# Down projection with seven products of halves in three chunks of its contraction, in one sequence with gate/up and the embedding gate

## The chip, the cores and the metric

The kernel runs on one core of a Trainium2 chip. The metric is the device time of one execution in microseconds; the time given for a kernel is the median of its runs.

## What is computed

One decoder layer over 2048 tokens with a model width of 1024, all in float32. The part that matters here is the end of the layer. `h` is the residual after attention and mLSTM, `rms_norm` scales by the root of the mean square and by a gain:

```python
D_MODEL = 1024; SEQ = 2048; PLE_DIM = 256
D_FF = ((8 * D_MODEL + 3 * 256 - 1) // (3 * 256)) * 256      # 2816
...
mix = jnp.concatenate([mla_out, mlstm_out], axis=-1) @ w_out[i]
h = h + rms_norm(mix, attn_post_norm[i])
f = rms_norm(h, ffn_pre_norm[i])
f = (jax.nn.silu(f @ w_gate[i]) * (f @ w_up[i])) @ w_down[i]
h = h + rms_norm(f, ffn_post_norm[i])
h = h + jax.nn.sigmoid(h @ w_ple_gate[i]) * (p[i] @ w_ple_proj[i])
```

## The kernel before, in words

Tensors lie transposed: rows of 128 features on the partitions, tokens along the free axis, in four blocks of 512 tokens (b = 0 to 3). Two blocks form a token pair: `tb = 1` is blocks 2 and 3, which goes first, `tb = 0` is blocks 0 and 1. A float32 product is made of three matmuls on halves of the mantissa (`mm3`, L133 to L138): each operand is split into `hi` (a cast on ScalarE, L128) and `lo` (a subtraction on VectorE, L124, the line of the helper `tt`), for weights in the tiles `wh`/`wl`, for activations in `xh`/`xl`. One matmul is 128x128 by 128x512.

Gate and up are made as a 2x2 block product with seven products in place of eight (Strassen's scheme in Winograd's form): `strassen`, L352. The two rows of the block are gate tile j and up tile j, the two columns the token blocks of the pair, and the contraction is cut in two halves of 512. `w_ops` (L323) loads the four quarters of the weights of one j into `wr` tiles and forms the seven weight operands; `lead_first` and `lead_second` (L279, L292) form the seven activation operands, four 128x512 tiles each, which stay for all 22 j. One product (`step`, L367) is 4 tiles x 3 = 12 matmuls. The methods `p1` to `p7` order the seven products of one j among those of its neighbours; the partial sums go out of PSUM into `ct` tiles by ScalarE (`copy`, L384) or are added by VectorE (`result`). Since the activation operands of a new token pair are not ready when it starts, the first j of each pair of token blocks is made with eight plain products (`straight_pair`, L474) while VectorE forms the others. `gate_up` (L1452) multiplies silu(gate) by up and writes the result to DRAM (`hf`).

After both token pairs comes the down projection in `phase3` (from L1328): for each of the four token blocks the 22 tiles of `hf` are loaded and split, and each of the 8 output tiles takes 22 x 3 = 66 matmuls with freshly loaded and split weights. `second_norm` (L1443) normalises a block and writes the new residual to DRAM (`h2`). Then `embed` (L1477) makes the sigmoid gate with the same seven products for each token pair (4 row pairs of w_ple_gate, the first of them straight), with the small projection of p between them.

`first_norm` (in `phase3`) makes `h1` of a block after the output projection; for blocks 0 and 1 its eight steps per block stand in `self.side`, a list from which `tick` (L224) takes one step after each product of the running sequence. So this work lies beside the first j of `gate_up(1)`.

The order of instructions on each engine is set when the program is built: a scheduler simulates the program and places each instruction on its engine's list, and each engine then runs its list in that order. Tiles come from pools with a fixed number of buffers per name (`SHARED`, `OWN`, L38 and L39: five `ld`, seven `ct`, six `acc`, two `tt`, one `sq`, four `wr`, seven `wh` and `wl`, 28 `xh` and `xl`); a tile's first writer waits until a buffer of that name is free. All loads and stores named here are issued by SP.

Of the kernel before, what the change touches and what calls it, by code (L numbers as in the profile page):

```python
# [17 lines left out]
P = 128  # L18
D = 1024
T = 2048  # L20
TB = 512
# [13 lines left out]
BUSY = 4  # L35
# [26 lines left out]
class Layer:  # L62
# [13 lines left out]
    def setup(self):  # L76
# [41 lines left out]
        self.hf = [dt([KF, P, TB], F32, name=f"hf{b}") for b in range(NB)]  # L118
        self.y2 = [dt([KD, P, TB], F32, name=f"y2_{b}") for b in range(NB)]
        self.h2 = [dt([KD, P, TB], F32, name=f"h2_{b}") for b in range(NB)]  # L120
# [134 lines left out]
    def load(self, src, alt=False, tag=None):  # L255
        t = self.tl(tag or ("ct" if alt else "ld"))
        self.nc.sync.dma_start(out=t, in_=src)
        return t
# [20 lines left out]
    def lead_first(self, get, spare=False):  # L279

        st = self.xs = {}
        self.help = "dve"
        self.raws = {}
        self.ops = [[] for _ in range(7)]
        for n, k in enumerate(LEAD):
            x = self.raws[k] = get(k, 0, "ct" if n > 5 else "xl" if n % 2 else "xh")
            st[k, 0] = self.x_pair(x, "dve")
            self.ops[0 if k < 4 else 2].append(st[k, 0])  # L290

    def lead_second(self, get):  # L292
# [9 lines left out]
        def sums(kk):  # L302
# [7 lines left out]
            ops[4].append(self.x_pair(t1, self.help))  # L310
            tt("dve", b21, b21, t2, ALU.subtract)
            ops[5].append(self.x_pair(b21, self.help))
# [10 lines left out]
    def w_ops(self, w1, w2, busy, first):  # L323
# [8 lines left out]
        help = self.help if busy else "dve"  # L332
        tt("dve", s1, a21, a22, ALU.add)
        o0 = self.w_pair(a11, lo_eng=help)
        o2 = self.w_pair(a12, lo_eng=help)
# [11 lines left out]
        o5 = self.w_pair(a22, lo_eng=help)  # L347
# [3 lines left out]

    def strassen(self, xo, pairs, emit, lead, place=None, late=False):  # L352


        nc, tt = self.nc, self.tt

        def ct():
            return self.tl("ct")

        def prod(ps, w, x, kk, start, stop, onto=False):  # L360
            s = slice(kk * P, (kk + 1) * P)
            self.mm3(ps, (w[0][:, s], w[1][:, s]), x[kk], start, stop, onto)

        self.straight_pair(*pairs[0], lead, emit, place)
        state, order = {}, [None]

        def step(j, i, bank, first=True):  # L367

            wo = state[j]["w"]
            with ExitStack() if order[0] is None else self.tc.issue_after(order[0]):  # L370
                for kk in range(4):
                    with self.paced():
                        prod(bank, wo[i], xo[i], kk, first and kk == 0, kk == 3, not first)
            order[0] = self.last("PE")
            with self.behind():
# [6 lines left out]
        def copy(bank, c=None):  # L382
            c = c or self.tl("ct")
            nc.scalar.copy(out=c, in_=bank)  # L384
            return c

        def done(j, i, t, c):
            state[j]["out"].append((i, t, c))
            if late and len(state[j]["out"]) < 4:
                return  # L390
            for i, t, c in state[j]["out"] if late else [(i, t, c)]:
                emit(j, i, t, c)

        def where(j, i, t, c=None):
            return place and place(j, i, t) or c or self.tl("ct")

        def result(j, i, t, bank, x):
            c = where(j, i, t, x)
            tt("dve", c, bank, x, ALU.add)
            done(j, i, t, c)  # L400

        def p1(j):
            s = state[j] = dict(w=self.w_ops(*pairs[j], j < BUSY, j == 1), out=[])
            s["a"] = self.bank()
            step(j, 0, s["a"])
            s["c1"] = copy(s["a"])

        def p2(j):
            s = state[j]
            bank = self.bank()  # L410
            step(j, 2, bank)
            result(j, 0, 0, bank, s["c1"])

        def p6(j):
            s = state[j]
            step(j, 1, s["a"], False)
            s["u2"] = copy(s["a"])

        def p5(j):
            s = state[j]  # L420
            s["b"] = self.bank()
            step(j, 4, s["b"])
            if "p3" in s:
                tt("dve", s["u2"], s["b"], s["u2"], ALU.add)
                result(j, 0, 1, s["p3"], s["u2"])

        def p7(j):
            s = state[j]
            step(j, 3, s["a"], False)
            s["u3"] = copy(s["a"])  # L430
            if "b" in s:
                result(j, 1, 1, s["b"], s["u3"])

        def p4(j):
            s = state[j]
            step(j, 5, s["a"], False)
            done(j, 1, 0, copy(s["a"], where(j, 1, 0)))

        def p3(j):
            s = state[j]  # L440
            if "b" in s:
                step(j, 6, s["b"], False)
                result(j, 0, 1, s["b"], s["u2"])
            else:
                s["p3"] = self.bank()
                step(j, 6, s["p3"])


        final = len(pairs) - 1
        for f in (p1, p2, p3, p6, p5, p7):  # L450
            f(1)
        for j in range(2, final + 1):
            p1(j)
            p2(j)
            p4(j - 1)
            p6(j)
            if j < final:
                p5(j)
            if j > 2:
                p3(j - 1)  # L460
            p7(j)
# [4 lines left out]
        s = state[final]  # L466
        result(final, 1, 1, s["b"], s["u3"])
# [862 lines left out]
    def phase3(self):  # L1330
        nc, a, V = self.nc, self.a, self.vecs
        st = ExitStack()
        with st:
# [4 lines left out]
            self.h2_done = set()  # L1338
# [52 lines left out]
            def ready(b, r):  # L1391
                rf[b] = r
                if b >= 2:
                    self.lead_first(scaled(1), True) if b == 2 else self.lead_second(scaled(1))
# [9 lines left out]
            self.gate_up(1, self.ops, self.xs)  # L1404
# [201 lines left out]
```

## Time and profile before

| | |
|---|---|
| median of 3 runs | 2758.14 us (2758.07 to 2763.62) |
| profiled execution, its own time | 2755.9 us |
| its span | 2754.1 us |
| granted TensorE clock, mean | 0.983 |
| TensorE matmul busy | 2633.2 us, 96% of the span, 12307 instructions |
| VectorE busy | 1815.0 us, 66%, 3355 instructions |
| ScalarE busy | 1314.5 us, 48%, 2585 instructions |
| DMA | 386.93 MB, mean 140 GB/s |

A busy share is the time that instructions of an engine ran, over the span. Matmuls overlap in the pipeline, so their durations don't add up; how many start in a stretch is the better measure. The share of DMA is the mean busy share of the core's 16 DMA engines.

### The profile page before, as it was taken

To read this page: it belongs to the slowest core of one execution; us is meant where nothing else is said; L and a number is where in the kernel's file an instruction comes from. 1 tells how busy PE (TensorE), PEld (TensorE's weight loads), DVE (VectorE), ACT (ScalarE), POOL (GpSimd) and SP (SyncE) were. 2 spreads that over 40 slices of the span, in tenths; PEclk is the share of its full clock that TensorE was granted. 3 is DMA by queue.
4 is the path that set the end of the run, shared out by engine and by line. 5 is a ranking of instruction groups with operands and counts; after the bars stand their busy time and mean duration, and the time that the engine had idled before them with its cause. 6 is when DMAs were issued, how large, how long until landed. Compare 5 with 4: busy or idle time off the path is not lost.

```text
span 2754.1 us, 36357 instructions
## 1 busy us (share of the span) xinstructions
PE 2633.2 (96%) x12307; PEld 2183.3 (79%) x12307; DVE 1815.0 (66%) x3355; ACT 1314.5 (48%) x2585; POOL 185.6 (7%) x393
## 2 busy tenths in 40 slices
PE   7799889999999999999999989999999999999999
PEld 6678668778888878878888877888888888888777
DVE  8987877566666653898555585555573454646996
ACT  5565565466555543465333354433352334434463
POOL 0010010244333100000000000000000000000000
PEclk9899999999999999999999999999999999999999
DMA  4345354743432144737222232222263565756552
GB/s 141 125 160 194 122 148 149 223 123 96 126 104 88 55 161 161 248 105 236 81 84 83 82 123 81 87 82 81 84 213 114 178 223 178 258 164 229 183 161 84
DMA packets 222822, 386.93 MB, mean 140 GB/s; under 512 B 26252, under 2 KB 39180, under 8 KB 222636
## 3 DMA queue, kind: packets, MB, share of 16 engines
q1 hardware_dynamic: 221292, 383.59, 42.9%
q8 instruction: 96, 1.57, 0.2%
q10 hardware_dynamic: 1344, 1.03, 0.1%
q14 instruction: 90, 0.74, 0.1%
HBM read 278.48 MB, written 106.04 MB: 140 GB/s over the span
## 4 chain that ended last, share of the span: by engine, by line
PE 79%; DVE 8%; DMA 7%; ACT 3%; issue 2%; POOL 1%; SPq 0%; DVEq 0%; POOLq 0%; ACTq 0%
PE ps L136 22%; PE ps L137 22%; PE ps L138 22%; PE ps_t L1300 2%; DMA wr<-g_rd 1%; DVE xl L124 1%; PE ps_o L137 1%; DVE ct L124 1%; DVE wl L124 1%; PE ps_s L1260 1%; PE ps_o L138 1%; PE ps_o L136 1%; PE ps_s L1261 1%; PE ps_s L1262 1%; PE ps_s L1263 1%
## 5 line engine op out<-in xcount | busy, mean ns | idle before, releaser
L136 PE MATMUL ps<-xh,wh 128*128 128x512 f32 x3000 | 1175.0, 395 | 49.2 <-ACT xh L128 18.6
L137 PE MATMUL ps<-xl,wh 128*128 128x512 f32 x3000 | 1178.9, 393 | 5.0 <-DVE xl L124 4.1
L138 PE MATMUL ps<-xh,wl 128*128 128x512 f32 x3000 | 1177.0, 393 | 0.0
L136 PEld LDWEIGHTS ps<-xh,wh 128*128 128x128 f32 x3000 | 569.3, 190 | 174.9 <-ACT xh L128 22.4
L137 PEld LDWEIGHTS ps<-xl,wh 128*128 128x128 f32 x3000 | 569.7, 190 | 125.3 <-DVE xl L124 5.9
L138 PEld LDWEIGHTS ps<-xh,wl 128*128 128x128 f32 x3000 | 569.2, 190 | 119.9 <-DVE wl L124 0.3
L124 DVE TENSOR_TENSOR wl<-wr,wh 128x512 fp32r<-128x512 f32 x575 | 387.0, 675 | 400.8 <-ACT wh L128 396.1
L128 ACT CAST wh<-wr 128x512 fp32r<-128x512 f32 x575 | 348.2, 608 | 632.8 <-PE ps L137 492.2
L124 DVE TENSOR_TENSOR ct<-ps,ct 128x512 f32<-128x512 f32 x174 | 120.0, 690 | 133.8 <-PE ps L138 127.8
L384 ACT COPY ct<-ps 128x512 f32<-128x512 f32 x248 | 144.0, 580 | 29.1 <-PE ps L138 21.8
L128 ACT CAST wh<-st 128x512 fp32r<-128x512 f32 x128 | 78.6, 620 | 163.4 <-PE ps L137 142.4
L128 ACT CAST xh<-ld 128x512 fp32r<-128x512 f32 x164 | 99.8, 621 | 64.4 <-DMA ld<-hf 28.8
L1311 DVE TENSOR_TENSOR acc<-ps_t,acc 128x512 fp32r<-128x512 f32 (+2 forms) x144 | 91.8, 643 | 53.3 <-ACT acc L1310 52.8
L1268 DVE TENSOR_REDUCE mx<-ps_s 128x1 f32<-128x512 f32 (+3 forms) x160 | 96.9, 608 | 35.6 <-PE ps_s L1264 33.4
L124 DVE TENSOR_TENSOR xl<-ld,xh 128x512 fp32r<-128x512 f32 x152 | 102.8, 690 | 20.4 <-ACT xh L128 19.6
L1310 ACT CAST acc<-ps_t 128x512 fp32r<-128x512 f32 (+2 forms) x144 | 78.0, 551 | 70.5 <-PE ps_t L1300 68.7
L1278 ACT ACTIVATE xl<-ps_s,mn 128x512 f32<-128x512 f32 (+3 forms) x144 | 90.3, 633 | 39.7 <-DVE mn L1274 23.0
L124 DVE TENSOR_TENSOR wl<-st,wh 128x512 fp32r<-128x512 f32 x128 | 87.7, 689 | 24.3 <-ACT wh L128 24.3
L1300 PE MATMUL ps_t<-ident,xl 128*128 128x128 f32 x544 | 88.3, 277 | 0.3 <-DVE acc L1311 0.3
L124 DVE TENSOR_TENSOR acc<-acc,sq 128x512 f32<-128x512 f32 x102 | 70.4, 691 | 12.9 <-ACT sq L249 12.4
L1300 PEld LDWEIGHTS ps_t<-ident,xl 128*128 128x128 f32 x544 | 68.6, 143 | 11.4 <-DVE acc L1311 0.5
L1260 PE MATMUL ps_s<-xh,wh 128*128 128x512 f32 (+2 forms) x160 | 66.8, 418 | 7.4 <-ACT xl L1278 7.2
(317 smaller groups left out, 3035.0 us busy)
## 6 DMA issues: line engine op xcount, KB each, us to landing
wr<-w_down SPq DMA_DIRECT2D x160, 256.0 KB, 2.9
wr<-w_gate SPq DMA_DIRECT2D x88, 256.0 KB, 2.8
wr<-w_up SPq DMA_DIRECT2D x88, 256.0 KB, 2.8
hf<-ct SPq DMA_DIRECT2D x88, 256.0 KB, 2.0
ld<-hf SPq DMA_DIRECT2D x88, 256.0 KB, 4.3
wr<-w_in SPq DMA_DIRECT2D x80, 256.0 KB, 3.1
y<-ct SPq DMA_DIRECT2D x64, 256.0 KB, 2.2
ld<-y SPq DMA_DIRECT2D x56, 256.0 KB, 4.1
```

Source lines behind the costliest of these rows:

```text
L124: (self.nc.gpsimd if eng == "pool" else self.nc.vector).tensor_tensor(out=out, in0=x, in1=y, op=op)
L128: self.nc.scalar.copy(out=hi, in_=src)
L136: mm(out, w[0], x[0], start=start, stop=False)
L137: mm(out, w[0], x[1], start=False, stop=False)
L138: mm(out, w[1], x[0], start=False, stop=stop)
L384: nc.scalar.copy(out=c, in_=bank)
L1260: mm(o, qn[0][:, qs], kn[c][0][:, :n], start=True, stop=False)
L1268: v.tensor_reduce(mx[:, j, c:c + 1], s_ps[:, :w], axis=AX.X, op=ALU.max, negate=True)
L1278: nc.scalar.activation(out=p[:, :x.shape[1]], in_=x, func=AF.Exp, bias=top, accum_out=sm[:, j, c:c + 1])
L1300: nc.tensor.transpose(t_ps[:, j * P:(j + 1) * P], pt[j, kt // 4][:, kc], self.ident)
L1310: nc.scalar.copy(out=ph[:, b0:], in_=t_ps[:, c0:])
L1311: v.tensor_tensor(pl[:, b0:], t_ps[:, c0:], ph[:, b0:].bitcast(F32), ALU.subtract)
```

## The change

- Down projection: the 22 contraction tiles are cut into three chunks of 2x3, 2x4 and 2x4 tiles (`CHUNKS`), and in each chunk two output tiles by two token blocks are made with seven products of halves. The 16 output tiles of a token pair stay in SBUF (`wr`, `ppl`, `ct`) over the three chunks, and the parts are added there.
- The weight operands of down and of the embedding gate are formed once (`w_sum`, 16 of them: 4 row pairs x 3 chunks of down, and 4 of w_ple_gate) and stored to DRAM as seven tiles each; each use loads them and splits them (`w_fed`). The 16 steps are appended to `self.side` before `gate_up(1)` starts.
- The activation operands of `gate_up(0)`, of down and of embed are formed once (`x_sums`) and stored to DRAM as seven tiles, with seven stores, in place of one store of each `hf`, `h2` tile; `fed` loads and splits them.
- `stream` runs gate/up of both token pairs, down of both (three jobs each) and embed of both as one sequence: while the last j of one job runs, the activation operands of the next are loaded, product by product. Only the first j of `gate_up(1)` is still made with eight plain products.
- `second_norm` becomes eight steps per token pair in `self.side`. The product of gate and up goes to `acc` (first token block) or `ppl` (second), not into the `ct` tile of the gate.
- `BUSY` and the variants of engine and spare go away without effect: both engines named were the same.

```diff
+CHUNKS = ((0, 3), (6, 4), (14, 4))
+FED = (0, 2, 1, 4, 3, 5, 6)
...
+    def w_sum(self, w1, w2, n, dst):
+        tt = self.tt
+        a11, a12, a21, a22 = (self.load(w[:, z * n:(z + 1) * n], n=n)[:, :n] for w in (w1, w2) for z in range(2))
+        s1, s2 = (self.tl("tt")[:, :n] for _ in range(2))
+        tt("dve", s1, a21, a22, ALU.add)
+        tt("dve", s2, s1, a11, ALU.subtract)
+        tt("dve", a21, a11, a21, ALU.subtract)
+        s4 = self.tl("sq")[:, :n]
+        tt("dve", s4, a12, s2, ALU.subtract)
+        for i, x in enumerate((a11, s2, a12, a21, s1, a22, s4)):
+            self.nc.sync.dma_start(out=dst[i][:, :n], in_=x)
+    def fed(self, hi, lo, src, n=TB):
+        hi, lo = self.tl(hi, F32R), self.tl(lo, F32R)
+        raw = lo.bitcast(F32)[:, :n]
+        self.nc.sync.dma_start(out=raw, in_=src)
+        self.nc.scalar.copy(out=hi[:, :n], in_=raw)
+        self.tt("dve", lo[:, :n], raw, hi[:, :n].bitcast(F32), ALU.subtract)
+        return hi, lo
+    def w_fed(self, src, n):
+        o = {i: self.fed("wh", "wl", src[i][:, :n], n) for i in FED}
+        return [o[i] for i in range(7)]
+    def x_sums(self, b11, b12, b21, b22, dst, t3, t4):
+        tt, dma = self.tt, self.nc.sync.dma_start
+        t1, t2 = self.tl("tt"), self.tl("tt")
+        dma(out=dst[0], in_=b11)
+        dma(out=dst[2], in_=b21)
+        dma(out=dst[6], in_=b22)
+        tt("dve", t1, b12, b11, ALU.subtract)
+        dma(out=dst[4], in_=t1)
+        tt("dve", t2, b22, t1, ALU.subtract)
+        dma(out=dst[1], in_=t2)
+        tt("dve", t3, b22, b12, ALU.subtract)
+        dma(out=dst[3], in_=t3)
+        tt("dve", t4, b21, t2, ALU.subtract)
+        dma(out=dst[5], in_=t4)
...
             order[0] = self.last("PE")
+            if id(jb) in after and j == len(jb["pairs"]) - 1:
+                feed(after[id(jb)], i)
             with self.behind():
                 self.tick()
...
+    def part(m, i, t, bank):
+            if not jb["sums"]:
+                c = self.tl("ct")
+                nc.scalar.copy(out=c, in_=bank)
...
             self.until(lambda: 3 in rf)
-            self.gate_up(1, self.ops, self.xs)
-            self.until(lambda: 1 in rf)
-            self.lead_first(scaled(0))
-            self.lead_second(scaled(0))
-            self.gate_up(0, self.ops, self.xs)
-            for b in (2, 3, 0, 1):
-                xs = [self.x_pair(self.load(self.hf[b][k])) for k in range(KF)]
...
+            self.side += self.weight_sums()
+            jobs = [self.gate_up(1, xo=self.ops, lead=self.xs),
+                    self.gate_up(0, feed=lambda i: [x[i] for x in self.h1op],
+                                 ready=lambda: self.h1_done == 4)]
             for tb in (1, 0):
...
+                jobs += self.down(tb)
+            self.stream(jobs + [self.embed(tb) for tb in (1, 0)])
...
                 s, u = half.pop((j, 0, t)), half.pop((j, 1, t))
-                self.tt("dve", s, u, s, ALU.mult)
-                nc.sync.dma_start(out=self.hf[2 * tb + t][j], in_=s)
...
+                x = got[j, t] = self.tl("ppl" if t else "acc")
+                self.tt("dve", x, u, s, ALU.mult)
+                m = j // 2
+                quad = [(k, z) for k in (2 * m, 2 * m + 1) for z in range(2)]
+                if all(i in got for i in quad):
+                    b = [got.pop(i) for i in quad]
+                    self.x_sums(*b, self.hfop[tb][m], b[1], self.tl("sq"))
...
+        def half(kk, z):
+            for t in range(2):
+                k, b = 4 * z + kk, 2 * tb + t
+                y, h = self.load(self.y2[b][k], tag="ld"), self.load(self.h1[b][k], tag="acc" if tb else "st")
+                nc.vector.scalar_tensor_tensor(y, y, V[:, 32 + k:33 + k], self.r2[tb, t], ALU.mult, ALU.mult)
+                self.tt("dve", y, y, h, ALU.add)
+                got[z, t] = y
+            if z:
+                b = [got[z, t] for z in range(2) for t in range(2)]
+                nc.sync.dma_start(out=self.h2op[tb][kk][7], in_=b[1])
+                self.x_sums(*b, self.h2op[tb][kk], self.tl("st"), self.tl("st"))
+                self.h2_done[tb] += 1
+        self.side += [lambda kk=kk, z=z: half(kk, z) for kk in range(4) for z in range(2)]
```

### What the change moves

Three places matter. All are at the start of `gate_up(1)`, where j = 3 and j = 4 of gate/up are under way. Numbers behind names tell tiles of one name apart; a line of the changed kernel differs from that of the one before (its L133 and L129 are the split's L128 and L124, its L456 the copy's L384, its L251 the first square of `square_sum`, L246).

**ScalarE, before.** The copy `ct_13101<-ps_13005` takes the second partial sum of j = 3 out of PSUM, before TensorE may go on into the same bank with the product `p7` of j = 3:

```order
L128 CAST wh_13188<-wr_13177 128x512
L249 ACTIVATE sq_12884<-ld_12877 128x512
L384 COPY ct_13075<-ps_12815 128x512
L128 CAST wh_13192<-wr_13179 128x512
L384 COPY ct_13101<-ps_13005 128x512
L249 ACTIVATE sq_12910<-ld_12903 128x512
```

**ScalarE, now.** The same copy is `ct_13509<-ps_13413`; `ld_13129` is the first tile of `first_norm` of block 0:

```order
L133 CAST wh_13609<-st_13593 128x512
L1544 ACTIVATE ct_13321<-ct_13321 128x512
L251 ACTIVATE acc_13105<-ld_13129 128x512
L456 COPY ct_13509<-ps_13413 128x512
L254 ACTIVATE sq_13159<-ld_13152 128x512
L254 ACTIVATE sq_13229<-ld_13222 128x512
L133 CAST wh_13614<-wr_13589 128x512
```

The copy now stands behind the first square of `first_norm` of block 0, which before came fifteen rows ahead of it.

**VectorE, now.** Behind the lower half of the fourth weight operand of j = 4 (`wl_13610`) come 41 rows of `w_sum` in a row, of the sixth sum to the last, without any other instruction between them. This is their end (`ld_13080`, `ld_13082`, `ld_13076`, `ld_13078` are the four quarters of the last sum):

```order
L129 TENSOR_TENSOR sq_13055<-ld_13044,tt_13050 128x512
L129 TENSOR_TENSOR tt_13084<-ld_13080,ld_13082 128x512
L1456 SCALAR_TENSOR_TENSOR ld_13129<-ld_13129,vecs_67,acc_13103 128x512
L129 TENSOR_TENSOR tt_13085<-tt_13084,ld_13076 128x512
L129 TENSOR_TENSOR ld_13080<-ld_13076,ld_13080 128x512
L129 TENSOR_TENSOR ld_13129<-ld_13129,ppl_13131 128x512
L129 TENSOR_TENSOR sq_13089<-ld_13078,tt_13085 128x512
L129 TENSOR_TENSOR tt_13286<-ppl_12911,acc_12684 128x512
L129 TENSOR_TENSOR acc_13283<-ct_13281,ct_12990 128x512
```

The tile that the first square of `first_norm` reads is written behind 43 of the 44 rows of the last eleven sums, and so is the product of gate and up of j = 1 (`acc_13283`), which frees two `ct` tiles.

**SP, now.** The eleven DMAs of one weight sum, as they stand in the middle of those eleven sums (a sum's seven stores and four loads of its neighbours; no load for gate/up is among them):

```order
L262 DMA ld_12782<-w_down 128x512
L262 DMA ld_12784<-w_down 128x512
L262 DMA ld_12812<-w_down 128x512
L365 DMA w_sums_down2_1_171<-ld_12780 128x512
L365 DMA w_sums_down2_1_171<-ld_12784 128x512
L365 DMA w_sums_down2_2_172<-ld_12812 128x512
L365 DMA w_sums_down2_1_171<-tt_12786 128x512
L365 DMA w_sums_down2_1_171<-tt_12787 128x512
L365 DMA w_sums_down2_1_171<-ld_12782 128x512
L262 DMA ld_12814<-w_down 128x512
L365 DMA w_sums_down2_1_171<-sq_12791 128x512
```

This group of eleven repeats; the four loads of each sum go through the five `ld` buffers, which the stores of the sum before must give back.

## Rows read from the trace of the kernel before

**Rows 1.** The page's engines and slices: busy share in 40 slices of 69 us.
```profile
span 2754.1 us, 36357 instructions
PE   7799889999999999999999989999999999999999
DVE  8987877566666653898555585555573454646996
PEclk9899999999999999999999999999999999999999
DMA  4345354743432144737222232222263565756552
```

**Rows 2.** Windows in gate/up and down: stretch, busy us (and instructions) by engine, clock, DMA.
```profile
1400.00:1450.00 50.00, 50.00 (x222) 41.40 (x222) 28.12 (x44) 19.88 (x35) 0.00 (x0) 1.00 0.25 84
1500.00:1550.00 50.00, 50.00 (x222) 41.42 (x221) 28.11 (x44) 19.53 (x34) 0.00 (x0) 1.00 0.25 82
2050.00:2100.00 50.00, 50.00 (x222) 41.43 (x221) 23.06 (x37) 18.46 (x32) 0.00 (x0) 1.00 0.56 177
2160.00:2560.00 400.00, 400.00 (x1787) 331.83 (x1786) 224.13 (x388) 153.03 (x267) 0.00 (x0) 1.00 0.63 205
```

**Rows 3.** Windows from the first token pair of gate/up to the second.
```profile
1600.00:1650.00 50.00, 42.77 (x180) 34.31 (x179) 44.63 (x72) 25.90 (x46) 0.00 (x0) 0.97 0.35 116
1650.00:1700.00 50.00, 45.00 (x188) 36.43 (x188) 30.67 (x49) 19.70 (x34) 0.00 (x0) 0.93 0.23 79
1655.00:1660.00 5.00, 3.44 (x8) 2.51 (x8) 4.29 (x8) 2.36 (x5) 0.00 (x0) 0.50 0.20 64
1660.00:1665.00 5.00, 5.00 (x22) 4.04 (x21) 1.89 (x3) 1.48 (x3) 0.00 (x0) 0.94 0.06 17
```

**Rows 4.** Windows of the embedding, to 4 us before the end.
```profile
2550.00:2600.00 50.00, 46.53 (x205) 37.46 (x203) 47.23 (x85) 24.27 (x44) 0.00 (x0) 1.00 0.50 159
2600.00:2650.00 50.00, 47.59 (x202) 38.98 (x203) 41.54 (x68) 26.09 (x47) 0.00 (x0) 0.97 0.74 241
2650.00:2700.00 50.00, 47.59 (x201) 38.47 (x200) 48.35 (x81) 30.72 (x56) 0.00 (x0) 0.97 0.38 123
2700.00:2750.00 50.00, 47.91 (x211) 39.12 (x209) 30.06 (x46) 18.87 (x33) 0.00 (x0) 1.00 0.15 56
```

**Rows 5.** Timeline of DVE, back to back.
```profile
1208.35 0.69 DVE L124 TENSOR_TENSOR wl<-wr,wh 128x512 fp32r<-128x512 f32 x1
1208.95 0.69 DVE L124 TENSOR_TENSOR tt<-ct,tt 128x512 f32<-128x512 f32 x1
1209.55 0.70 DVE L124 TENSOR_TENSOR ld<-ct,ld 128x512 f32<-128x512 f32 x1
```

**Rows 6.** Five of the 10 us windows with busiest DMA.
```profile
1090.00:1100.00 10.00, 10.00 (x46) 8.28 (x45) 5.61 (x10) 4.14 (x8) 0.00 (x0) 1.00 1.03 373
1130.00:1140.00 10.00, 10.00 (x46) 8.29 (x45) 7.08 (x11) 4.71 (x8) 0.00 (x0) 1.00 1.04 387
1240.00:1250.00 10.00, 10.00 (x46) 8.29 (x45) 9.07 (x16) 5.75 (x11) 0.00 (x0) 1.00 1.03 348
1250.00:1260.00 10.00, 10.00 (x46) 8.29 (x45) 10.00 (x17) 6.21 (x11) 0.00 (x0) 1.00 1.04 357
2370.00:2380.00 10.00, 10.00 (x46) 8.29 (x45) 6.80 (x11) 3.31 (x6) 0.00 (x0) 1.00 1.00 360
```

**Rows 7.** Timeline of PE: the statistics of blocks 0 and 1 among j = 1.
```profile
1206.34 1.84 PE L162 MATMUL psx<-rmean,acc 128*128 128x1 f32 x16
1208.05 0.49 PE L137 MATMUL ps<-xl,wh 128*128 128x512 f32 x1
```

**Rows 8.** The window of 50 us at the start of gate/up.
```profile
1200.00:1250.00 50.00, 50.00 (x234) 41.78 (x233) 46.87 (x96) 28.89 (x52) 0.00 (x0) 1.00 0.45 151
```

**Rows 9.** The chain that ended last, of the second norm: a store, then a load.
```profile
2575.24 2.01 DMA h<-ld
2577.32 3.39 DMA ld<-y
2580.73 0.75 DVE ld L1447
2594.82 3.33 DMA h<-ld
```

**Rows 10.** The page's DMA issues: KB each, us from issue to landing.
```profile
hf<-ct SPq DMA_DIRECT2D x88, 256.0 KB, 2.0
ld<-y SPq DMA_DIRECT2D x56, 256.0 KB, 4.1
```

More of the change, by code (lines that the diff above doesn't have):

```diff
@@ L397, in result @@
[L397 to L403, printed above, removed]
+        def part(m, i, t, bank):
+            jb, j = seq[m]
+            if not jb["sums"]:
+                c = self.tl("ct")
+                nc.scalar.copy(out=c, in_=bank)
+                state[m][i, t] = c
+                return
+            kind, tiles = jb["sums"]
+            if kind == "first" and (j, i, t) not in tiles:
+                c = tiles[j, i, t] = self.tl("wr" if j == 0 else "ppl" if j == 1 or (j, i, t) == (3, 1, 0) else "ct")
+                nc.scalar.copy(out=c, in_=bank)
+            else:
+                c = tiles[j, i, t]
+                tt("dve", c, bank, c, ALU.add)
@@ L404, in p1, with p2 @@
+        def p1(m):
+            jb, j = seq[m]
+            if j == 0 and jb["begin"]:
+                jb["begin"]()
+            s = state[m] = dict(w=jb["weights"](j, m == 0), out=[])
             s["a"] = self.bank()
[L405 to L409, printed above, removed]
+            step(m, 0, s["a"])
+            part(m, 0, 0, s["a"])
+        def p2(m):
             bank = self.bank()
-            step(j, 2, bank)
-            result(j, 0, 0, bank, s["c1"])
@@ L427, in p7 @@
[L427 to L430, printed above, removed]
-            if "b" in s:
[L432 to L440, printed above, removed]
+                x = s[0, 1]
+                tt("dve", x, s["b"], x, ALU.add)
+                whole(m, 0, 1, s["p3"])
@@ new lines, in down, with emit @@
+    def down(self, tb):
+        nc, tiles, accs, got = self.nc, {}, {}, {0: 0, 1: 0}
+        def emit(j, i, t, c):
+            b = 2 * tb + t
+            nc.sync.dma_start(out=self.y2[b][2 * j + i], in_=c)
+            if t not in accs:
+                accs[t] = self.acc_tile()
+            self.square_sum(accs[t], c, got[t] == 0, tag="tt")
+            got[t] += 1
+            if got[t] == KD:
+                self.rms_later(accs[t], 1024, lambda r: self.second_norm(tb, t, r))
+        jobs = []
+        for c, (k0, n) in enumerate(CHUNKS):
+            pairs = [self.down_pair(j, k0, n) for j in range(KD // 2)]
+            jobs.append(self.job(
+                pairs, emit, n=n, sums=("last" if c == 2 else "more" if c else "first", tiles),
+                weights=lambda j, first, c=c, n=n: self.w_fed(self.w_sums[f"down{c}", j], n * P),
+                feed=lambda i, k0=k0, n=n: [x[i] for x in self.hfop[tb][k0 // 2:k0 // 2 + n]]))
+        return jobs
@@ L1500, in steps, with begin @@
             turn = ((0, 0), (1, 0), (1, 1), (0, 1)) if j == 0 else ((0, 0), (1, 1), (1, 0), (0, 1))
[L1501 to L1504 removed]
+            return [lambda: weight(j)] + [lambda n=n, t=t: ahead(n, t) for n, t in turn]
+        def begin():
+            self.side += [lambda t=t, k=k: embed_in(t, k) for t in range(2) for k in range(2)] + steps(0)
         def emit(j, n, t, c):
```

284 lines of the change are left out of this document (158 added, 126 removed).

## Prediction

> **What bounds the kernel now.** I read the page first, then windows by stage, then the order of both programs. TensorE is busy from the start of the last third to the end at the full granted clock while VectorE and DMA have room [rows 1]. In a steady stretch of gate/up or of down 222 matmuls start in 50 us, so one costs 50/222 = 0.2252 us, and no other engine is near its limit [rows 2]. TensorE's list of matmuls is the bound there: a matmul that is left out is 0.2252 us off the time. It loses time at two places. Between the token pairs of gate/up 180 + 188 matmuls start in 100 us where 444 would fit, 76 x 0.2252 = 17.1 us, part of it at the lower clock after the gap (0.50, then 0.94) [rows 3]. In the embedding 819 start in 200 us where 888 would fit, 15.5 us, and the last row of windows stops 4 us before the end [rows 4].
>
> The sum is made against the profiled execution's own 2755.9 us, which is 2.2 us under the median of the runs, 2758.14.
>
> **What goes.** Down took 4 blocks x 8 tiles x 66 matmuls = 2112; now 2 token pairs x 4 row pairs x 7 products x 11 tiles x 3 = 1848, which is 264 fewer. Three first j lose their eighth product (`gate_up(0)` and both embeddings), 3 x 12 = 36. Together 300, at 0.2252 us **-67.6 us**. The gap between the token pairs goes almost wholly, since the operands of the next job are loaded during the last j of this one: **-15** of 17.1 [rows 3]. Of the embedding's 15.5 us [rows 4] I take **-12**; the tail of the last outputs stays. Without anything added: 2755.9 - 94.6 = 2661.3 us.
>
> **What is added beside TensorE.** VectorE's list from the first operand of down to the end of down holds 212 full and 28 three-quarter operations for the first token pair and 266 and 28 for the second. Back to back one takes 0.60 us [rows 5], so 142 and 174 us against 924 x 0.2252 = 208 us of matmuls per pair: covered on the whole, cost nothing, but with little room. If that cover were gone VectorE would set the pace of down. In gate/up it is busy 28 of 50 us [rows 2], and `x_sums` adds 4 operations per two j, 2.4 us in 38: covered. DMA in down and second norm is 63 MB in 208 us for the second token pair, 303 GB/s on the mean, where the busiest windows carried 348 to 387 at a share of 1.00 to 1.04 [rows 6]: covered on the mean, not in its bursts.
>
> **The weight sums: the term that decides.** The 16 steps of `w_sum` are in the side list ahead of `first_norm` of blocks 0 and 1 and come within 16 products. Buffers of one name are given out in program order as I read the lists, so the first `ld` and `acc` tiles of `first_norm` come behind all sums, and the `acc` tile for the product of gate and up of j = 1 behind those; its two `ct` tiles stay taken meanwhile. The scheduler's lists show the result: on ScalarE the copy that frees the bank for `p7` of j = 3 stands behind the first square of `first_norm`, and on VectorE that square's input stands behind 43 of the 44 operations of the last eleven sums. So TensorE can't start `p7` of j = 3 before nearly all sums are made. Nothing remains for it ahead of that: `wl_13610`, which stands on VectorE right before the eleven sums, needs a buffer that `p3` of j = 2 gives back, the product before `p7`. Behind the waiting copy are queued the casts of the weights of j = 4, and SP has no load for j = 5 but one until the sums are through.
>
> When would TensorE get there? Its list is the same up to the start of j = 1. The statistics at 1206.34 to 1208.05 us [rows 7] stand in the middle of its first product; from there 17 products and 2 matmuls, 206 x 0.2252 = 46.4 us, lead to about 1255 us. In the trace of before nothing waits there [rows 8].
>
> How long do eleven sums take? Two bounds. By volume: from the second load of the sixth sum to the last load of the sixteenth SP has 114 DMAs, 29.9 MB; at 387 to 348 GB/s [rows 6] 77 to 86 us. By the chain of a buffer: a load 3.39 to 4.1, three operations of 0.60 until the third quarter may be stored, a store 2.0 to 3.33 [rows 5, 9, 10], 7.2 to 9.2 us for one sum, since four of the five `ld` buffers go round in each; ten rounds are 72 to 92. Both limits act on the same transfers, so I take 8.5 us a round, near the upper end because the latencies in those rows were met at less than full DMA: 85 us, and 5 for the first sum's and the last sum's own operations and the square and copy behind them. **+90 us**, ends 72 and 105 (ten rounds of 10).
>
> The page "DMA: Bandwidth & Descriptors" of the Trainium skill, section Bandwidth, speaks against this change: it gives 138 GB/s for transfers of 64 KB and 341 for 1 MB and asks for 1 MiB or more, which for the 256 KB pieces here would put the rate between the two and make these 29.9 MB an estimated 88 to 217 us. The trace doesn't agree: with several in flight the same pieces ran at 348 to 387 [rows 6], so the rows decide. The same section has 425 GB/s for 16 MB, by which the stall would be some 70 us; no row here reaches that.
>
> **Smaller terms.** After such a gap the clock comes back as in [rows 3], +2 us. Then VectorE has the 16 steps of `first_norm` and the products that piled up, beside j = 4 and 5; before, the same steps lay there with VectorE busy 46.87 of 50 us [rows 8] and no gap: +6, ends 0 and 15. `second_norm` of the first token pair lies under chunks 0 and 1 of the second pair's down: 101 DMAs, 26.1 MB, with 18 weight operands among them; 73 us at 357 GB/s, against 198 matmuls, 44.6 us, and one row pair loaded ahead, 14 us: **+15**, ends 0 and 30. The other five changes of operands: 28 loads, casts and subtractions beside 14 products, 11 MB in 38 us, 290 GB/s: +6 in all, ends 0 and 20. `second_norm` of the second token pair must end before the last embedding starts: 102 DMAs, 26.7 MB, 75 us, against some 53 us of matmuls after its second statistic: **+15**, ends 5 and 25.
>
> Sum: 2661.3 + 90 + 2 + 6 + 15 + 6 + 15 = **2795.3**, I say 2795 us, 1.3% over the median. With all low ends 2661.3 + 72 + 2 + 0 + 0 + 0 + 5 = 2740; with all high ends 2661.3 + 105 + 2 + 15 + 30 + 20 + 25 = 2858.
>
> **The rivals.**
> *A, the sums are quick.* If loads and stores run ahead far enough, the eleven sums go at VectorE's pace: 44 x 0.60 = 26 us, and the time is 2661.3 + 26 + 44 = 2731; with the smaller terms at their low ends too, 2661.3 + 26 + 7 = 2694. It decides when the block takes less than 94.6 - 44 = 51 us, 4.6 us a sum. For it: DMA was idle for half of this stretch [rows 8], so the first five sums may be done early. Against: 4.6 us a sum are 2.88/4.6 = 626 GB/s, which no row comes near. Faster than before; 0.16, of which I see more near 2730 than below.
> *B, transfers slower than the busiest windows.* If a sum's stores and loads wait for each other through the five buffers, so that a round takes 12 us, the eleven cost 10 x 12 + 5 = 125 and the later bursts their upper ends, 2661.3 + 125 + 2 + 15 + 30 + 20 + 20 = 2873. For it: a single store and load of the chain in [rows 9] already take 5.4 to 6.7 us. Against: [rows 6]. The Trainium skill's rule on small transfers, above, would bring it about. 0.12.
> *C, VectorE becomes the bound of down.* 174 of 208 us leaves 16% for waits in its list; if the starts of its operations came 0.69 us apart, the duration of each row, and not 0.60 [rows 5], it were 200 of 208, and every change of operands would show: +25 over my sum, 2820, inside the upper part of the range. 0.10.
> *D, the change doesn't do what it says.* The lists hold 11955 matmuls before and 11655 now, 300 fewer, so this can only be a cancellation of terms within 0.2%: 0.05.
>
> **How the numbers follow.** The forecast case has 0.57, and 2740 to 2858 is its own range. 0.2% of 2758, 5.5 us, is about what a measurement of this kernel can tell from no change. Faster by more than that (under 2752.6): all of A, and 0.04 of the low ends of the forecast: 0.20. Within: 0.06. Slower: 0.74. For 8 in 10 I go down to 2722, into A, and leave out half of it, and up to 2855, and leave out B: low 2722, high 2855.
>
> **What would show it.** Right: in the changed trace TensorE has one gap of 70 to 105 us that starts near 1255, behind a copy of ScalarE; in it VectorE runs nothing but sums, with idle time put down to loads of w_down, and DMA is at 320 GB/s or more; matmuls number 300 fewer; between the token pairs of gate/up there is no gap over 2 us; gaps of 5 to 25 us stand in the first chunks of the second down and before the last embedding. Wrong: no gap, or one under 50 us near 1255 (then A), or many small gaps through down behind VectorE (then C), or a DMA share under 0.7 in the gap (then the buffers' turn, not the volume, sets the sums' time).

## The result: 3.2% slower, where 1.3% was forecast

| | before | after |
|---|---|---|
| median of 4 runs, us | 2758.11 | 2847.92 |
| ratio of after to before, 95% interval | | 1.0321 (1.0303 to 1.0339) |
| profiled execution, its own time, us | 2755.9 | 2848.03 |
| granted TensorE clock, mean | 0.983 | 0.954 |

The sign and the range (2722 to 2855) held; the size did not: +90 us against a forecast of +37. One run of e4_spread_both, below, took 7278.87 us; the numbers given for that kernel are of its other three.

The profile after, engines and slices of 71 us (to be read against [rows 1]), and the largest group of matmuls with its idle time:

```profile
span 2846.3 us, 36993 instructions
PE 2577.8 (91%) x12007; PEld 2131.6 (75%) x12007; DVE 1966.4 (69%) x3612; ACT 1365.1 (48%) x2670; POOL 185.3 (7%) x393
PE   7899889899999999960699999999999999799969
PEclk9899999999999999985799999999999999899979
DMA  4346354734332157489864236333327567967984
L141 PE MATMUL ps<-xh,wh 128*128 128x512 f32 x2900 | 1142.0, 396 | 194.7 <-ACT ct L456 126.9
```

The 300 matmuls are gone (12007 for 12307). Three holes have come into TensorE's row of slices, each where DMA stands at 8 or 9. What TensorE waited for, from 1100 us to the end (releaser: us in total, times, longest):

```profile
PE ps L141 <- ACT ct L456: 124.0, 2, 107.4
PE ps L141 <- ACT xh L372: 17.1, 2, 15.8
PE ps L141 <- ACT wh L372: 16.3, 2, 10.2
PE psx L141 <- ACT sq L133: 11.8, 2, 8.2
...
PE ps L143 <- DVE wl L129: 1.3, 2, 1.0
```

And the windows of these stretches, with one window between the token pairs of gate/up for comparison (columns as in [rows 2]):

```profile
1250.00:1300.00 50.00, 6.25 (x28) 4.85 (x26) 18.49 (x30) 3.49 (x7) 0.00 (x0) 0.59 0.95 324
1300.00:1350.00 50.00, 0.00 (x0) 0.00 (x0) 14.50 (x23) 0.00 (x0) 0.00 (x0) 0.50 0.92 313
1350.00:1400.00 50.00, 19.76 (x67) 15.69 (x68) 35.57 (x57) 12.83 (x22) 0.00 (x0) 0.65 0.94 321
1700.00:1750.00 50.00, 50.00 (x222) 41.42 (x221) 39.94 (x65) 30.83 (x56) 0.00 (x0) 1.00 0.67 225
2400.00:2450.00 50.00, 33.36 (x127) 25.67 (x127) 40.32 (x66) 20.41 (x36) 0.00 (x0) 0.83 0.99 363
2450.00:2500.00 50.00, 48.96 (x216) 40.18 (x215) 34.11 (x54) 16.44 (x27) 0.00 (x0) 1.00 0.70 251
2650.00:2700.00 50.00, 46.79 (x198) 38.39 (x199) 41.92 (x67) 23.41 (x40) 0.00 (x0) 0.97 0.96 333
2700.00:2750.00 50.00, 24.68 (x78) 17.76 (x77) 32.24 (x50) 22.46 (x38) 0.00 (x0) 0.66 0.90 313
```

Count what is missing against 222 matmuls in 50 us, at 0.2252 us each. 1250 to 1400: 666 - 95 = 571, **128.6 us**. 2400 to 2500: 101, **22.7 us**. 2650 to 2750: 168, **37.8 us**. Together 189.1. With the 67.6 us of matmuls left out and the 17.1 and 15.5 us that the old gaps cost [rows 3, 4], 2755.9 - 100.2 + 189.1 = 2844.8, against 2848.03 measured; 3.2 us are not placed. Between the token pairs nothing is lost any more.

The first hole is the forecast one. It starts at 1256.2 us (forecast: about 1255), behind the copy L456. Of its 107.4 us, 9.8 pass before the block of eleven sums begins, since the fifth sum starts only at 1256.02, when its loads have landed, and the sixth a round later, at 1266.02; 91.9 are the ten rounds, from 1266.02 to 1357.93; 5.7 the end.

### The profile page after: what moved, and what is told of

The parts are those of the page before. It is cut to its first block, busy times and chain, and to the rows that moved or that the text cites. A ratio compares the mean times of both kernels' runs of the same rounds, so it can differ in the third digit from the quotient of the medians.

```text
span 2846.3 us, 36993 instructions
## 1 busy us (share of the span) xinstructions
PE 2577.8 (91%) x12007; PEld 2131.6 (75%) x12007; DVE 1966.4 (69%) x3612; ACT 1365.1 (48%) x2670; POOL 185.3 (7%) x393
## 4 chain that ended last, share of the span: by engine, by line
PE 74%; DMA 12%; DVE 8%; ACT 2%; issue 2%; SPq 1%; POOL 1%; DVEq 0%; POOLq 0%; ACTq 0%
PE ps L141 20%; PE ps L143 20%; PE ps L142 20%; DMA ld<-w_down 2%; PE ps_t L1390 2%; DMA wr<-g_rd 1%; DVE wl L129 1%; DVE xl L129 1%; PE ps_o L142 1%; PE ps_s L1350 1%; PE ps_o L143 1%; PE ps_o L141 1%; PE ps_s L1351 1%; PE ps_s L1352 1%; PE ps_s L1353 1%
## 5 line engine op out<-in xcount | busy, mean ns | idle before, releaser
L142 PE MATMUL ps<-xl,wh 128*128 128x512 f32 x2900 | 1141.8, 394 | 3.5 <-DVE xl L129 2.2
L143 PE MATMUL ps<-xh,wl 128*128 128x512 f32 x2900 | 1140.5, 393 | 1.4 <-DVE wl L129 1.3
L133 ACT CAST wh<-wr 128x512 fp32r<-128x512 f32 x346 | 214.1, 620 | 341.9 <-PE ps L142 214.7
L129 DVE TENSOR_TENSOR wl<-wr,wh 128x512 fp32r<-128x512 f32 x346 | 237.1, 687 | 173.7 <-ACT wh L133 169.9
L129 DVE TENSOR_TENSOR ct<-ps,ct 128x512 f32<-128x512 f32 x244 | 167.3, 686 | 124.7 <-PE ps L143 119.8
L372 ACT CAST wh<-wl 128x512 fp32r<-128x512 f32 (+1 forms) x224 | 132.1, 594 | 207.8 <-DMA wl<-w_sums_down 109.1
L129 DVE TENSOR_TENSOR wl<-wl,wh 128x512 fp32r<-128x512 f32 (+1 forms) x224 | 144.8, 654 | 109.2 <-ACT wh L372 106.4
L129 DVE TENSOR_TENSOR xl<-xl,xh 128x512 fp32r<-128x512 f32 x256 | 168.9, 685 | 28.0 <-ACT xh L372 27.0
L372 ACT CAST xh<-xl 128x512 fp32r<-128x512 f32 x238 | 144.0, 620 | 67.6 <-DMA xl<-hfop 26.9
L133 ACT CAST wh<-st 128x512 fp32r<-128x512 f32 x118 | 72.5, 621 | 173.9 <-PE ps L142 143.2
L456 ACT COPY ct<-ps 128x512 f32<-128x512 f32 x201 | 116.7, 581 | 16.1 <-PE ps L143 12.9
L129 DVE TENSOR_TENSOR wl<-st,wh 128x512 fp32r<-128x512 f32 x118 | 80.5, 684 | 15.6 <-ACT wh L133 15.5
L1544 ACT ACTIVATE ct<-ct 128x512 f32<-128x512 f32 x88 | 55.6, 632 | 46.8 <-DVE ct L129 46.5
```

The lines of the kernel that those rows point to most:

```text
L129: (self.nc.gpsimd if eng == "pool" else self.nc.vector).tensor_tensor(out=out, in0=x, in1=y, op=op)
L133: self.nc.scalar.copy(out=hi, in_=src)
L142: mm(out, w[0], x[1], start=False, stop=False)
L143: mm(out, w[1], x[0], start=False, stop=stop)
L372: self.nc.scalar.copy(out=hi[:, :n], in_=raw)
```

## The experiments

All kernels below are the changed one with an edit, and were run beside the kernel before on the same chip (its median there 2749.9 to 2752.6 us), so ratios to before are compared. In units of before, 0.001 is 2.75 us; the changed kernel stands at 1.0321.

### The place of the sums: e1_spread and e2_dense_behind

```diff
                     self.side += [lambda kk=kk: self.h1_sums(kk, rf) for kk in range(4)]
+                    for f in self.weight_sums():
+                        self.side += [f] + [lambda: None] * 6
...
-            self.side += self.weight_sums()
```

> The 16 weight sums stand behind first_norm and h1_sums in the side list, one every seven products of gate/up. Theory (their place ahead of first_norm makes TensorE wait for nearly all of them): the gap of 571 missing matmuls (128.6 us) between 1250 and 1400 us goes, and the time is 2848 - 129 = 2719 us, 2705 to 2740. Rival 'the added traffic costs it wherever it stands': SP has 323 DMAs in some 15 j there, 84 MB in 284 us, 296 GB/s; if that is too much the gap only spreads: 2820 to 2850 us. Rival 'VectorE': many waits of 0.5 to 1 us behind wl, 2740 to 2800 us.

2717.59 us, ratio 0.9871 (0.9853 to 0.9888). The same stretch, in windows:

```profile
1250.00:1300.00 50.00, 50.00 (x226) 41.52 (x225) 48.46 (x85) 25.17 (x45) 0.00 (x0) 1.00 0.75 250
1300.00:1350.00 50.00, 50.00 (x230) 41.48 (x230) 41.57 (x80) 19.01 (x34) 0.00 (x0) 1.00 0.65 227
1350.00:1400.00 50.00, 49.05 (x217) 40.30 (x216) 40.53 (x69) 18.60 (x34) 0.00 (x0) 1.00 0.89 300
```

The hole is gone with all transfers still made. The rival that the traffic costs it anywhere falls: at 300 GB/s beside it TensorE loses 5 of 222 starts, and 3 and 6 in the next two windows of 50 us.

For e2_dense_behind the edit is the same without the empty steps.

> The 16 weight sums stand behind first_norm and h1_sums, but in one piece, one per product. SP's list then has 223 DMAs, 57 MB, beside seven j of gate/up, 132 us. Theory (what counts is that TensorE's way leads through the sums; beside running j they cost only what their volume takes beyond the cover): 57 MB at 313 to 350 GB/s are 163 to 182 us against 132, so a stall of 30 to 50 us spread over this stretch, 2735 to 2785 us, most likely 2755. Rival 'order alone, density is nothing': 2719 as with the spread sums. Rival 'the traffic costs the same anywhere': 2848.

2765.33 us, ratio 1.0042 (1.0029 to 1.0055). One wait is left, near 1500 us:

```profile
PE ps L141 <- ACT ct L456: 49.7, 3, 46.4
```

So place and density both count: behind `first_norm` the block costs 48 us instead of 129, spread it costs about nothing.

### What sets a round: e3_stubs, e5_copies, e8_pool_stores

A round of the block took 9.19 us (91.9 / 10). One round in the chain that ended last, changed kernel, with the piece that stands before it (start, us, what; short pieces left out):

```profile
1308.85 3.28 DMA w_sums_down<-ld
...
1312.15 0.70 DVE tt L129
...
1313.49 0.69 DVE ld L129
...
1314.20 0.34 SPq L365
...
1314.59 0.59 SPq L262
...
1315.23 0.63 SPq L365
...
1315.96 0.45 SPq L262
...
1316.45 4.68 DMA ld<-w_down
...
1321.21 0.70 DVE tt L129
```

The third operation of the sum ends at 1314.18, 2.03 us after the first began. Then SP issues two stores and two loads in its order, and 2.27 us later the last load that the next sum reads. It lands after 4.68 us, and the next sum begins. The landing times in the trace say the same of all ten rounds: 2.2 to 2.9 us from the third operation's end until that load is issued, 4.2 to 5.1 us until it lands, and the sum begins at most 0.13 us later.

For five of the ten sums the profile names a store as what ended the wait, as in the first line for the sum at 1312.15. That store landed at 1313.36, when the sum had begun; the sum's last load landed at 1312.07. In the other four of the five, too, the store landed over 1 us after the sum began. In the ten rounds SP waited for stores of the sums before a load 7 times, 1.8 us in all. So stores are next to nothing in the turn, where the chain of a buffer in the prediction (load, operations, store) had 2.0 to 3.33 us for one. That the round meets the upper end of that chain, 9.2 us, is a coincidence. At the same time DMA is busy at 0.92 to 0.95. Three edits separate the volume, the stores and SP's order.

```diff
         for i, x in enumerate((a11, s2, a12, a21, s1, a22, s4)):
-            self.nc.sync.dma_start(out=dst[i][:, :n], in_=x)
+            m = 32 if i in (0, 2, 5) else n
+            self.nc.sync.dma_start(out=dst[i][:, :m], in_=x[:, :m])
```

> As the changed kernel, but of the seven stores of a weight sum the three of plain quarters (a11, a12, a22) carry 32 columns in place of 384 or 512, and the products that would read these quarters read the sum s2 in their place, so the weights of three of the seven products are left out. The chain of the buffers stays (each quarter still has a store to wait for), the volume of a round falls from 11 pieces to 8.2. Theory 'volume sets the round of 9.19 us': 6.9 us a round, ten rounds and what stands around them some 25 us less, 2848 - 25 = 2823 us (2815 to 2830). Rival 'the turn of the five ld buffers (load, three operations, store) sets the round': 8.5 to 9.2 us a round, 2840 to 2848 us.

2829.18 us, ratio 1.0276 (1.0261 to 1.0292), 12 us less by the ratios. Ten rounds from 1254.06 to 1342.30 us, 8.82 us each. The time is in the range of the theory, the rounds are in that of its rival: the ten rounds are 3.7 us of the gain, and TensorE's second wait for the copy, 11.0 us instead of 16.6, another 5.6.

e5_copies makes the three plain stores copies within DRAM (here, too, the weights of three of the seven products are left out):

```diff
+        for i in (0, 2, 5):
+            self.nc.sync.dma_start(out=dst[i][:, :m], in_=prev[1][:, :m])
```

> As the changed kernel, but the three stores of plain quarters in a weight sum are copies from DRAM to DRAM (of the s2 tile of the sum before, so the weights of three of the seven products are left out): eleven pieces of 256 KB a round as before, but the ld buffers of three quarters are free as soon as VectorE has read them. e3_stubs left the volume's part away and its rounds came down from 9.19 only to 8.82 us at a DMA share of 0.76, so the turn of the buffers is now the theory: load 3.4 to 4.8 us, up to three operations of 0.6, then the next load, 6 to 7 us a round, the gap near 1255 us shorter by 20 to 35 us, 2815 to 2830 us where the changed kernel had 2848. Rival 'volume': 9.2 us a round, 2840 to 2855 us.

2834.09 us, ratio 1.0306 (1.0289 to 1.0323), not told apart from the 1.0321 of the changed kernel. Ten rounds from 1260.61 to 1349.77, 8.92 us each, the last nine 8.77. The expectation of 6 to 7 was wrong. In e8_pool_stores all seven stores are `self.nc.gpsimd.dma_start`.

> As the changed kernel, but the seven stores of each weight sum are issued by GpSimd's queue, so that the loads of the next sum no longer stand on SP behind stores that wait for VectorE. Neither a quarter less volume (8.82 us a round at 245 GB/s) nor buffers free without a store (8.77) took more than 0.4 us off the round of 9.19. Theory 'SP's order is the third part of the round: the last load stands behind the stores of four operations': a buffer's own turn is a load 4.1 and a store 3.3 and about 1 us of issue, five buffers for four loads, 6.7 to 7.6 us, the volume of 2.88 MB at 350 to 390 GB/s 7.4 to 8.2: rounds of 7.4 to 8.2 us, the time 2830 to 2840 us where the changed kernel had 2848. Rival 'the DMA engines are at their rate for this mix already (302 to 343 GB/s)': 9.2 us, 2845 to 2855 us. Rival 'GpSimd issues slower than SP': longer, 2860 us and more.

2844.78 us, ratio 1.0332 (1.0312 to 1.0353): no gain. Ten rounds from 1262.05 to 1359.19, 9.71 us each, the last seven 9.93. Windows inside the block, e3_stubs, e5_copies and e8_pool_stores:

```profile
1256.00:1342.00 86.00, 0.00 (x0) 0.00 (x0) 25.16 (x40) 0.63 (x1) 0.00 (x0) 0.50 0.77 247
```
```profile
1271.00:1349.00 78.00, 0.00 (x0) 0.00 (x0) 23.12 (x36) 0.00 (x0) 0.00 (x0) 0.50 0.96 328
```
```profile
1290.00:1359.00 69.00, 0.00 (x0) 0.00 (x0) 17.80 (x28) 0.00 (x0) 26.37 (x49) 0.50 0.84 290
```

With a quarter of the volume gone the rounds are 4% shorter and DMA idles a quarter of the time: volume does not set the round. With the stores of three quarters gone from the turn of their buffers (e5_copies) they are 3% shorter, so those stores don't either. The chain of e8_pool_stores, where SP issues no stores:

```profile
1299.33 0.70 DVE tt L129
...
1301.36 0.61 DVE sq L129
...
1301.98 0.33 SPq L262
...
1302.40 6.22 DMA ld<-w_down
...
1308.75 0.70 DVE tt L129
```

A sum's fourth operation ends, a buffer comes free, the loads of the next sum go out, and it waits for the last of them. With five `ld` buffers and four loads in a sum, that load cannot be far ahead. Here SP's part is down to 0.4 to 0.8 us, but the load itself takes 6.2 to 7.3 us in the last seven rounds. In the last nine of e3_stubs and e5_copies it is 1.8 to 2.5 us of SP's issue and a load of 4.6 to 5.8 and 4.0 to 4.7 us. So the turn of operations, issue and load sets the round in all four kernels. Why a load takes so long in it, with a quarter of the volume gone as well, stays open. Whether more buffers would shorten the round was not tried.

### The second norm of the first token pair: e4_spread_both and e7_wider

```diff
-        self.side += [lambda kk=kk, z=z: half(kk, z) for kk in range(4) for z in range(2)]
+        for kk in range(4):
+            for z in range(2):
+                self.side += [lambda kk=kk, z=z: half(kk, z)] + [lambda: None] * (6 if tb else 0)
```

> As e1_spread, and the eight steps of the second norm of the first token pair also stand one every seven products of down of the second pair, not one per product. Theory (its 101 DMAs in one burst make the gap of some 22 us between 2400 and 2500 us): that gap goes, 2719 - 20 = 2699 us, 2690 to 2715, about 20 us under e1_spread; the gap before the last embedding, some 38 us, stays. Rival 'down itself is too dense in DMA or on VectorE for the norm anywhere': as e1_spread.

2701.84 us, ratio 0.9823 (0.9799 to 0.9846), 13 us under e1_spread by the ratios. Between 2250 and 2350 us, where e1_spread misses 101 matmuls (22.7 us), 40 are missing. So the burst made most of this hole; 9 us of it stay. e7_wider has 13 empty steps between the weight sums and 8 here.

> As e4_spread_both, but one weight sum in fourteen products instead of seven, and one step of the second norm of the first token pair in nine instead of seven. What is left there by the windows of e4_spread_both: some 15 matmuls missing between 1400 and 1500 us and some 40 between 2250 and 2350 us, 12 us. Theory (these come from the density): 4 to 9 us less, 2695 to 2700 us. Rival (they come from the change of operands at the start of down(0), and the sums beside it): 2702 to 2706.

2699.0 us, ratio 0.9823 (0.9803 to 0.9843), and 2699.17, 0.9810 (0.9796 to 0.9824) when run again: not told apart from e4_spread_both by the time. By the windows the wider spacing helps a little: 27 matmuls are missing between 2250 and 2350 us in place of 40, and none between 1400 and 1500 us in place of 12.

### The gap before the last embedding: e6, e9, e10, e11

e6_small_h loads `h1` of the last two blocks in 32 columns (`n=m`, `m = TB if tb else 32`) and leaves out the rest of their residual; it is made from e4_spread_both.

> As e4_spread_both, but in the second norm of the second token pair the residual h1 is loaded and added in 32 of 512 columns only (the rest of the residual of these two blocks is left out): 16 pieces of 256 KB less, 4.2 MB, the same number of buffers and turns. The gap before the last embedding is some 38 us of matmuls in e4_spread_both, at a DMA share of 0.93 and 325 GB/s. Theory 'volume sets it': 4.2 MB at 325 GB/s, 12 us less, 2692 us (2688 to 2697). Rival 'turns of the st and ld buffers set it': 0 to 4 us less, 2700 to 2705 us.

2697.15 us, ratio 0.9801 (0.9787 to 0.9816), not told apart from e4_spread_both; the 12 us of the theory 'volume' did not come. e9_pool_norm is e7_wider with `half`'s loads and stores for the second token pair issued by `nc.gpsimd`.

> As e7_wider, but the loads and stores of the second norm of the second token pair are issued by GpSimd's queue. In e7_wider its four groups of sums end near 2503, 2521, 2547 and 2564 us, and SP waits 28.6 us of 2530 to 2640 for TensorE to give back buffers of weight operands. Theory 'SP's order holds the norm up': the groups come every 16 to 18 us, the gap of 159 missing matmuls (36 us) between 2500 and 2650 us gets 10 to 20 us shorter, 2680 to 2689 us. Rival 'volume' (share of DMA 0.86 to 1.02 in the gap): 0 to 5 us less, 2694 to 2699 us. Rival 'GpSimd issues slower': 2700 us and more.

2706.08 us, ratio 0.9829 (0.981 to 0.9849): wrong, no gain. e10_no_residual is e7_wider without `h = self.load(self.h2op...)` in `emit` for the first token pair; it adds the gate's product a second time, and the residual is left out.

> As e7_wider, but the embedding of the first token pair adds the gate's product a second time in place of the residual, so its 16 loads of h2op through the five ld buffers are left out: 4.2 MB less in the stretch before the last embedding, as in e6_small_h, but here 16 turns of the ld buffers go too, which the loads of the second norm share. 159 matmuls (36 us) are missing between 2500 and 2650 us in e7_wider and e4_spread_both, 135 in e6_small_h. Theory 'the ld buffers, which the norm shares with the embedding, hold it up': 12 to 25 us less, 2674 to 2687 us. Rival 'volume alone, as in e6_small_h': 4 to 8 us less, 2691 to 2695 us. Rival 'neither (the way from the last sum to the first operand and the weight of the small projection sets it)': 0 to 3 us less.

2684.36 us, ratio 0.9745 (0.9729 to 0.9762). TensorE from 2500 to 2650 us in e7_wider, e6_small_h, e9_pool_norm and e10_no_residual:

```profile
2500.00:2650.00 150.00, 122.02 (x503) 97.98 (x502) 105.87 (x164) 73.53 (x127) 0.00 (x0) 0.90 0.84 291
```
```profile
2500.00:2650.00 150.00, 127.22 (x527) 101.30 (x526) 102.28 (x170) 76.50 (x134) 0.00 (x0) 0.91 0.82 278
```
```profile
2500.00:2650.00 150.00, 115.92 (x487) 92.41 (x487) 102.93 (x164) 69.77 (x124) 28.98 (x54) 0.89 0.82 286
```
```profile
2500.00:2650.00 150.00, 133.10 (x563) 108.02 (x562) 109.15 (x172) 76.79 (x137) 0.00 (x0) 0.93 0.82 280
```

The same 4.2 MB are worth 24 matmuls in e6_small_h (23 against the 504 of e4_spread_both) and 60 in e10_no_residual, but the second norm is hardly faster in either: the last operation of its four groups of sums starts near 2503, 2520, 2546 and 2564 us in e7_wider and within 3 us of that in both. So the time of e10_no_residual is in the range of its theory, but the theory, that the norm is held up by the `ld` buffers, is wrong. What went is TensorE's second wait. The waits in this stretch, e7_wider and then e10_no_residual:

```profile
PE ps L141 <- ACT xh L372: 16.0, 2, 15.6
PE psx L141 <- ACT sq L133: 11.8, 2, 9.2
```
```profile
PE ps L141 <- ACT xh L372: 14.4, 1, 14.4
```

In e7_wider the chain runs from the end of the norm through the loads of operands to the weight of the small projection, which TensorE needs for its next product:

```profile
2565.90 5.30 DMA xl<-h2op
...
2571.22 5.93 DMA xl<-h2op
...
2577.17 5.40 DMA ld<-w_ple_proj
...
2582.59 0.63 ACT sq L133
...
2583.26 0.80 PE psx L141
```

So e11_early_weight loads that weight earlier:

```diff
-            return [lambda: weight(j)] + [lambda n=n, t=t: ahead(n, t) for n, t in turn]
+            return [lambda n=n, t=t: ahead(n, t) for n, t in turn] + [lambda: weight(j + 1)] * (j < last)
...
-            self.side += [lambda t=t, k=k: embed_in(t, k) for t in range(2) for k in range(2)] + steps(0)
+            self.side += [lambda t=t, k=k: embed_in(t, k) for t in range(2) for k in range(2)] + [lambda: weight(0)] + steps(0)
```

> As e7_wider, but the weight of the small projection for j + 1 is loaded and split right after the four projections of j, some seven products earlier, so that its load no longer stands on SP behind the last loads of operands for the last embedding. e10_no_residual took 60 missing matmuls (13.5 us) off the stretch 2500 to 2650 us while the four groups of sums of the second norm ended at the same times (2503, 2520, 2546, 2564 us): what went was the second wait, 11.8 us of TensorE behind the split of this weight. Theory 'that wait is only a load that stands too late': 8 to 12 us less, 2687 to 2691 us, the wait for sq gone, that for xh stays near 16 us. Rival 'e10's gain was volume and turns of ld': 0 to 3 us less, or the wait moves to xh as in e9_pool_norm: 2696 to 2702 us.

> The same as e7_wider, beside e11_early_weight on one chip: 2699 us (2695 to 2704), ratio to before 0.982.

2687.09 us, ratio 0.9755 (0.9741 to 0.9769), 12 us under e7_wider on the same chip. The waits of TensorE from 1100 us, first two lines; the line for `sq` is gone:

```profile
PE ps L141 <- ACT xh L372: 18.1, 2, 16.0
PE ps L143 <- DVE wl L129: 4.3, 3, 2.7
```

It computes all that the changed kernel does, and beats both: 2.4% under before, 5.5% under the change as made (0.9755 / 1.0321).

## Why the prediction was right in sign and short in size

The profiled execution is 52.7 us over the sum of 2795.3: 30.6 in the first hole, 7.7 and 22.8 at the two second norms, 3.2 not placed, less the 6 forecast for changes of operands, which have no hole of their own, and 5.6 for old gaps that went further than forecast.

- **300 matmuls, 0.2252 us each: right**, and the gaps that it expected to go went by the balance above (32.6 us where it took 27). Without new holes the sum stood at 2661 on a before of 2755.9; e11_early_weight has 2687 on one of 2752.6, with 16 us of wait before the last embedding left.
- **The stall of the weight sums: mechanism right, shown by e1_spread; size short.** This is the step that failed most: "+90", "+2 clock" and "+6" for `first_norm` are 128.6 us. Of the 30.6 us, 6.9 are the rounds, 9.2 us where I took 8.5. Here the chain itself was wrong: it had the landing of a store in it, for which no sum waited, left out SP's issue of 2.2 to 2.9 us, and took 3.39 to 4.1 us for a load that took 4.2 to 5.1. That its upper end fits is luck. 10.5 us stand around the rounds (9.8 + 5.7 where I had 5): I let the block start when TensorE gets to its wait, and the sums were a round late. The other 13.2 are behind the stall, where 21.2 us stand against my 8: TensorE waits a second time, 16.6 us, for the copy that stands on ScalarE behind squares of `first_norm`, whose loads come late at full DMA; and behind both waits the first matmuls start 0.43 us apart, at a granted clock of 0.50, which costs 4.6.
- **The DMA rate: too high.** The block ran at 313 to 324 GB/s, not at 348 to 387 [rows 6], which are bursts of 10 us. The estimate from the Trainium skill's "DMA: Bandwidth & Descriptors", section Bandwidth, was 88 to 217 us for this volume (its rows are of loads issued from GpSimd; here SP issues loads and stores); the ten rounds took 91.9, at its lower end, but for another reason: e3_stubs shows that the rate did not set them. The sign that I gave to tell volume from the buffers' turn, a DMA share under 0.7 in the gap, was no test: the share was 0.93, and the turn set the round all the same.
- **Second norm of the first pair, "+15": 22.7**, within its ends of 0 and 30. e4_spread_both shows that most of it is the burst.
- **Second norm of the second pair, "+15", ends 5 and 25: 37.8, outside.** The working gave 75 us for the norm by volume; in the changed kernel 85 passed from its first operation on VectorE, 2629.7, to the end of its last, 2714.9. And the working stopped there: behind the norm's end stand loads of operands and, behind those, the weight of the small projection, and TensorE restarts at half its clock (0.43 us a matmul; granted clock 0.66 on the mean from 2700 to 2750). The 12 us of wait for that weight were an order of loads, as e11_early_weight shows. What sets the norm's own pace, 61 us from the end of its first group of sums to that of the last, stays open: with 4.2 MB less it was 57 us (e6_small_h), without the `ld` turns of the embedding 61 again (e10_no_residual), with GpSimd's queue 79 (e9_pool_norm).
- **Other operand changes, "+6": next to nothing** for the one between the token pairs; the others lie inside the holes above and weren't separated.
- **The rivals.** A (quick sums) fell: 9.2 us a sum, not 4.6. B (a round of 12 us, 2873) named a longer turn of the buffers, the right direction and too far; the stores that it named were next to nothing. C fell: behind VectorE's `wl` TensorE waited 1.3 us from 1100 us to the end.

## What to carry to other kernels

Where steps of a side list share buffers that are given out in program order, a long dense block there is a wall: everything later in the list, and whatever that frees, stands behind it. Put it behind the steps that the main engine needs and one step per several products; here that turned +3.2% into -1.3% with the same transfers. When few buffers turn over, price the block by the turn that a trace shows (here operations, the issue of DMAs in their order, the load) and not by a DMA rate alone, check a releaser that the profile names against the landing times, and follow a stall on to the next thing that was loaded late behind it.

## What the runs showed that was not expected

- The time from issue to landing of the 256 KB load that a sum waits for differed between the kernels, and not with the rate: 4.2 to 5.1 us in the changed kernel (317 GB/s over its ten rounds), 4.6 to 5.8 in e3_stubs (247), 4.0 to 4.7 in e5_copies (328), 6.2 to 7.3 in e8_pool_stores (290).
- Cutting a quarter of a block's volume shortened its rounds by 4%, while DMA's share went from about 0.93 to 0.77.
- A releaser that the profile names can be wrong where two DMAs land close together: in five of ten rounds it named a store that landed over 1 us after the wait had ended.
- In the stall TensorE's granted clock fell to 0.50 (1.2 GHz) and stayed there until it worked again: 0.59 and 0.65 on the mean in the windows on its edges.
